# The second FFN's down product in another order: seven products, a weight sum by VectorE, a ring of its own for plain blocks, and later transposes

## The chip, the cores and the metric

The kernel runs on one core of a Trainium2 chip. The core has five engines that work side by side, each with an in-order queue of its own: TensorE (PE: matmuls; PEld is its loading of weights), VectorE (DVE), ScalarE (ACT), GpSimd (POOL) and SyncE (SP, which here only issues transfers). Sixteen DMA engines move data between the large memory and the on-chip memory; SP, ACT and POOL issue their transfers. The metric is the device time of one execution in microseconds (us), as the median of several runs.

## What is computed

Two layers of a diffusion backbone over 512 latent and 256 context tokens of width 1024, in float32. Each layer is a mixer (attention and linear recurrences) followed by a feed-forward network (FFN). The change is in the FFN of the second layer, in which only the 512 latent tokens are left. Cut to that:

```python
D_MODEL = 1024
SEQ = 512
D_FF = 2816

def _swiglu(h, w_gate, w_up, w_down):
    return (jax.nn.silu(h @ w_gate) * (h @ w_up)) @ w_down

def reference(...):
    ...
        h_lat = _modulate(_rms(x_lat, norm_pre_ffn[l]), m_lat[3], m_lat[4])
        x_lat = x_lat + m_lat[5] * _rms(_swiglu(h_lat, ffn_w_gate[l], ffn_w_up[l], ffn_w_down[l]), norm_post_ffn[l])
    ...
    return x_lat
```

## The kernel before

**Precision.** Every float32 operand of a matmul is split into a high part H (a cast by ScalarE to the matmul's reduced float32) and the rest L (a subtraction by VectorE). `mm3` then issues three matmuls, H·H, H·L and L·H. So each block of weights and of activations costs one ScalarE and one VectorE instruction before TensorE can use it.

**The second FFN** is `ffn_whole`. `first()` computes the first two columns of the gate and up products plainly, in two halves of 256 tokens (tiles "pearly"). While it does so, the last two token tiles are still being normed; their transposes wait in a list `self.turns`, and `self.turn(left)` issues transposes until `left` tiles are left. A tile's transposes are eight TensorE instructions (tile hT), each four followed by ScalarE's scale and shift and by the split into H and L. The tiles of the first half were transposed earlier, under the output projection; the two that wait belong to the second half of the tokens. After that, `seven` does the other gate and up products with a fast algorithm (seven products of half blocks in place of eight). The result is G, 512 tokens by 2816, in `np_` = 11 chunks of 2 times 128.

**The down product** is `down`: G (512 by 2816) times `w_down` (2816 by 1024), again with seven products of half blocks. A[r, k] are the four quarters of G (token half r, every other 128 rows k); B(k, j) those of the weights (half j of the columns). A[1, 0] has already had A[1, 1] taken off (`minus`). The products, each over 11 chunks, for two token tiles of 128 and 512 columns:

| name | activations (factor f) | weights (src) | bank before |
|---|---|---|---|
| 11 | A11 | B11 | X |
| N3 | A[0,0] as it then is, plus A12 | B22 | O |
| S1 | A21 − A22 | B11 + B12 | Q |
| SN | A21 − A22 − A11 | B11 + B12 + B22 | X, onto what 11 left |
| 22 | A22 | B11 + B12 + B22 + B21 | O |
| S3 | −A22 − (A21 − A22 − A11) | B12 + B22 | X, onto what 11 and SN left |
| 12 | A12 | B21 | Q |

The sums of weights are built in place in two tiles: `t` ("tb" in the profile) and `t3` ("tc"), each of 11 chunks of 512 columns. Where a sum grows, POOL issues an accumulating transfer (`add`, line 1707) from the large memory onto the tile, right after the operands of the product that used the old value were split. Plain blocks (N3, 12 and part of 11) go through a ring "raw" of three tiles that the whole kernel shares. The blocks of 11 for the first six chunks were loaded early (`early`).

The 11 chunks come in seven groups: two of one chunk, four of two, one of one. `operands(p, g)` makes H and L of weights and activations for a group; `ahead(3)` keeps three groups ready. The activations' ring (aH, aL) has three slots, that of the weights (wH, wL) four. After the last group of a product, each of its two output tiles is taken out of its bank into y, by ScalarE where it is the first term (`nc.scalar.copy`), by VectorE where it is added (`plus`, line 1761). `end` norms a finished token tile and stores it; `final` and `close` do the same for the last tile in two halves.

TensorE's matmuls in `down` and POOL's transfers there stay in the order of the program; what VectorE, ScalarE and SP do is ordered by a planner before the run, from the order of the program and from costs that it assumes. On the chip each queue is then in order.

Of the kernel before, what the change touches and what calls it, by code (L numbers as in the profile page):

```python
# [8 lines left out]
F32 = mybir.dt.float32  # L9
F32R = mybir.dt.float32r  # L10
# [3 lines left out]
ALU = mybir.AluOpType  # L14
# [3 lines left out]
P = 128  # L18
# [10 lines left out]
WU = 1024  # L29
# [104 lines left out]
class Attention:  # L134
# [7 lines left out]
    half = (slice(0, 64), slice(64, P))  # L142
# [174 lines left out]
class Net:  # L317
# [1295 lines left out]
    def ffn_whole(self, l, xp, yp, fp, pp, rp, h, ending):  # L1613


        nc, I = self.nc, self.I
        wg, wu, wd = I["ffn_w_gate"][l], I["ffn_w_up"][l], I["ffn_w_down"][l]
        tiles, n = h.order, h.n
        np_, nh = NFC // 2, n // P
        G = fp.tile([P, np_, 2, 2 * n], F32, tag="G", name="G")  # L1620

        self.banks(True)

        def go():
            return fp.tile([P, 2, 2 * n], F32, tag="go", name="go")

        def first():
            g = go()
            us = [[self.unit_cols(w, i * P) for w in (wg, wu)] for i in range(2)]
            h.open(xp)  # L1630
            for half in range(2):
                pm = self.mm_tile("pearly")
                pts = [[self.sc_tile("pearly", x)[:, :n] for x in range(2)], [pm[:, 512 * x : 512 * x + n] for x in range(2)]]
                tok = slice(n * half, n * half + n)
                for ks in ((range(4), range(4, 8)) if half == 0 else (range(8),)):
                    for i in range(2):
                        for m in range(2):
                            for k in ks:
                                self.mm3(pts[i][m], tuple(x[:, k, :] for x in us[i][m]), h.raw(k, half), k == 0, k == KD - 1)
                            if ks[0] == 0 and half == 0 and m == 0:  # L1640
                                self.turn(1 - i)
                for i in range(2):
                    nc.scalar.activation(g[:, i, tok], pts[i][0], AF.Silu)
                    nc.vector.tensor_tensor(G[:, 0, i, tok], g[:, i, tok], pts[i][1], op=ALU.mult)
                if half == 0:
                    pp.release()
                    tp = self.open_pool(f"t{l}")
                    h.sums(tp)
            h.late()
            return tp  # L1650

        tp = first()
        early = yp.tile([P, 8, 512], F32, tag="y", bufs=1, name="early")
        other = early[:, 6:8, :]
        self.blocks = wd.rearrange("(i k p) m -> k p i m", k=2, p=P)
        minus = lambda i: nc.vector.tensor_tensor(G[:, i, 0, n:], G[:, i, 0, n:], G[:, i, 1, n:], op=ALU.subtract)
# [24 lines left out]
        rp.release()  # L1681
        xp.release()
        dp = self.open_pool(f"d{l}")
        self.banks(None)
        y = self.down(dp, G, early, yp.tile([P, len(tiles), D], F32, tag="y", bufs=1, name=f"y{l}"), tiles, n, ending)
        return y

    def down(self, dp, G, early, y, tiles, n, ending):


        nc = self.nc
        np_, nh = NFC // 2, n // P
        B = lambda k, j, i: self.blocks[k][:, i, 512 * j : 512 * j + 512]
        A = {(r, k): G[:, :, k, n * r : n * r + n] for r in range(2) for k in range(2)}
        groups = [slice(0, 1), slice(1, 2)] + [slice(i, min(i + 2, np_)) for i in range(2, np_, 2)]
        ng = len(groups)
        v = nc.vector
# [6 lines left out]
        t = dp.tile([P, np_, 512], F32, name="tb")  # L1704
        t3 = dp.tile([P, np_, 512], F32, name="tc")
        end, final, follow = ending(y)
        add = lambda o, src: self.pin(nc.gpsimd.dma_start(out=o, in_=src, accum_op=ALU.add))
        load = lambda o, src: nc.sync.dma_start(out=o, in_=src)
        seven = (("11", "X"), ("N3", "O"), ("S1", "Q"), ("SN", "X"), ("22", "O"), ("S3", "X"), ("12", "Q"))

        def operands(p, g):
            i = groups[g]
            m = i.stop - i.start
            name = seven[p][0]
            H, L = [self.wp.tile([P, WU], F32R, tag=f"w{x}", bufs=4, name=f"w{x}")[:, : 512 * m].rearrange("p (i n) -> p i n", i=m) for x in "HL"]
            if name == "11":
                load(t[:, i], B(0, 0, i))
                if i.stop <= 6:
                    src = early[:, i]
            if name in ("N3", "12") or name == "11" and i.stop > 6:  # L1720
                src = self.wp.tile([P, WU], F32, tag="raw", bufs=3, name="raw")[:, : 512 * m].rearrange("p (i n) -> p i n", i=m)
                load(src, {"11": B(0, 0, i), "N3": B(1, 1, i), "12": B(1, 0, i)}[name])
            elif name != "11":
                src = (t3 if name == "S3" else t)[:, i]
            a = [x[:, :m] for x in (first.pop() if first else ring())]
            if name == "N3":
                f = dp.tile([P, 2, n], F32, tag="n3", bufs=2, name="n3")[:, :m]
                v.tensor_tensor(f, A[0, 0][:, i], A[0, 1][:, i], op=ALU.add)
            elif name == "S3":
                f = A[1, 1][:, i]  # L1730
                v.scalar_tensor_tensor(f, f, -1.0, A[0, 0][:, i], op0=ALU.mult, op1=ALU.subtract)
            else:
                f = A[{"11": (0, 0), "S1": (1, 0), "SN": (0, 0), "22": (1, 1), "12": (0, 1)}[name]][:, i]
            nc.scalar.copy(H, src)
            nc.scalar.copy(a[0], f)
            v.tensor_tensor(L, src, H.bitcast(F32), op=ALU.subtract)
            v.tensor_tensor(a[1], f, a[0].bitcast(F32), op=ALU.subtract)
            if name == "11":
                v.tensor_tensor(f, A[1, 0][:, i], f, op=ALU.subtract)
                add(t[:, i], B(0, 1, i))  # L1740
            elif name == "S1":
                add(t[:, i], B(1, 1, i))
                self.pin(nc.gpsimd.dma_start(out=t3[:, i], in_=B(0, 1, i)))
            elif name == "SN":
                add(t[:, i], B(1, 0, i))
                add(t3[:, i], B(1, 1, i))
            return a, (H, L)

        todo = [(p, g) for p in range(7) for g in range(ng)]
# [8 lines left out]
        out = {"X": [one(f"x{i}") for i in range(2)], "O": [one(f"o{i}") for i in range(2)]}  # L1758
        out["Q"] = [self.sc_tile("q", i) for i in range(2)]
        low, high = slice(0, 512), slice(512, D)  # L1760
        plus = lambda o, b, op=ALU.add: v.tensor_tensor(o, o, b, op=op)
        for p, (name, where) in enumerate(seven):
# [4 lines left out]
            for at, (g, i) in enumerate(order):  # L1767
# [3 lines left out]
                b = out[where][i]  # L1771
# [14 lines left out]
                y0, y1 = y[:, i, :], y[:, nh + i, :]  # L1786
                if name == "11":
                    nc.scalar.copy(y0[:, low], b)
                elif name == "N3":
                    nc.scalar.copy(y0[:, high], b)  # L1790
                elif name == "S1":
                    nc.scalar.copy(y1[:, high], b)
                    plus(y0[:, high], b)
                elif name == "SN":
                    plus(y0[:, high], b, ALU.subtract)
                elif name == "22":
                    nc.scalar.copy(y1[:, low], b)
                elif name == "S3":
                    plus(y1[:, low], b)
                    plus(y1[:, high], b, ALU.subtract)  # L1800
                    end(y1, tiles[nh + i])
                    if i == nh - 1:
                        close = final(dp, y0, tiles[i])
                else:
                    plus(y0[:, low], b)
                    if i < nh - 1:
                        end(y0, tiles[i])
                    else:
                        close()
# [304 lines left out]
```

## Time and profile before

| | us |
|---|---|
| median of three runs | 1743.5 (1741.79 to 1743.84) |
| the profiled execution's own time | 1742.7 |
| its span, first to last instruction | 1740.9 |
| TensorE busy | 1675.3 (96% of the span) |
| VectorE busy | 1298.3 (75%) |
| ScalarE busy | 896.4 (51%) |
| GpSimd busy | 108.6 (6%) |
| down product of the second FFN, first to last matmul | 1597.2 to 1733.1 |
| `first()` of the second FFN, first to last matmul | 1363.0 to 1394.5 |

How to read a row of the profile: a row of the time line gives start, duration, engine, line of the kernel, operation, the tile written <- the tiles read, their shape, and in brackets the idle time of the engine before it and what ended it. A row of the waits gives who waited for whom: us in total, times, the longest. A row by stretches gives the stretch, its length, the busy time (and instructions) of PE, PEld, DVE, ACT and POOL, the granted TensorE clock (1.00 is full speed), the mean busy share of the 16 DMA engines and GB/s. A group's row gives busy us, mean ns of one, and idle time before them. Matmuls overlap in the pipeline, so a row's duration is longer than the time from one start to the next.

### The profile page before, as it was taken

Reading aid. Unit: us, or ns where it says so; the run is one execution under the profiler, and the core shown is the slowest. Engines: PE = TensorE matmul, PEld = TensorE weight load, DVE = VectorE, ACT = ScalarE, POOL = GpSimd, SP = SyncE. Lnnn points to the kernel's source line nnn. Section 1 sums busy time; section 2 is a strip of 40 time slices with the busy share of each in tenths; the row PEclk is TensorE's granted clock in tenths of the full one; section 3 lists DMA queues with packets and bytes.
Section 4 is the critical chain, followed back from the end, with each engine's and each line's share of the span. In section 5 each row is a group of like instructions: output and inputs, shape, how many; then the busy total and the mean of one; then the engine's idle time right before and its main releaser. Section 6 shows DMA issues by size and latency. Waiting matters only on the chain.

```text
span 1740.9 us, 32512 instructions
## 1 busy us (share of the span) xinstructions
PE 1675.3 (96%) x13446; PEld 1500.4 (86%) x13446; DVE 1298.3 (75%) x2103; ACT 896.4 (51%) x1552; POOL 108.6 (6%) x128
## 2 busy tenths in 40 slices
PE   6999999999999999999999999999999999999887
PEld 5899987887999988999997888888887899998665
DVE  5889668835969999796668238887855789886667
ACT  4745567746442323333347346666644755554454
POOL 1004110000000000000001000000000000001240
PEclk9999999999999999999999999999999999999999
DMA  9641022134334455452235121211224253334993
GB/s 319 197 139 39 2 70 82 58 134 145 109 95 127 151 185 175 138 171 73 62 108 182 61 85 50 62 44 44 62 84 141 79 158 111 108 98 139 239 191 115
DMA packets 179680, 201.64 MB, mean 116 GB/s; under 512 B 7142, under 2 KB 141836, under 8 KB 179532
## 3 DMA queue, kind: packets, MB, share of 16 engines
q1 hardware_dynamic: 170704, 181.56, 33.3%
q0 software_dynamic: 6896, 14.42, 4.1%
q10 hardware_dynamic: 1932, 3.59, 0.7%
q8 instruction: 105, 1.72, 0.4%
q14 instruction: 43, 0.35, 0.1%
HBM read 190.08 MB, written 9.46 MB: 115 GB/s over the span
## 4 chain that ended last, share of the span: by engine, by line
PE 77%; DVE 9%; DMA 6%; ACT 4%; issue 2%; POOL 1%; SPq 0%; POOLq 0%; DVEq 0%; ACTq 0%
PE nat L355 12%; PE a L355 10%; PE acc L355 8%; PE ff L355 8%; PE E L355 7%; PE oproj L355 5%; PE D L355 3%; PE b L355 3%; PE fq L355 2%; PE gqk L355 2%; PE S L355 1%; PE pearly L355 1%; DMA tb<-in_ffn_w_down_dram 1%; DMA raw<-in_ffn_w_down_dram 1%; PE poh L355 1%
## 5 line engine op out<-in xcount | busy, mean ns | idle before, releaser
L355 PE MATMUL nat<-wH,x 128*128 128x256 f32 (+2 forms) x944 | 215.6, 318 | 3.0 <-ACT x L648 2.6
L734 ACT CAST wH<-raw 128x1024 fp32r<-128x1024 f32 x120 | 125.1, 1052 | 181.2 <-PE acc L355 54.1
L680 DVE TENSOR_TENSOR wL<-raw,wH 128x1024 fp32r<-128x1024 f32 (+1 forms) x104 | 124.3, 1203 | 82.5 <-ACT wH L679 81.6
L355 PEld LDWEIGHTS nat<-wH,x 128*128 128x128 f32 x944 | 157.6, 190 | 18.5 <-ACT x L648 3.6
L735 DVE TENSOR_TENSOR wL<-raw,wH 128x1024 fp32r<-128x1024 f32 x120 | 145.9, 1220 | 30.4 <-ACT wH L734 30.0
L679 ACT CAST wH<-raw 128x1024 fp32r<-128x1024 f32 (+1 forms) x104 | 106.8, 1038 | 81.1 <-PE nat L355 23.7
L355 PE MATMUL nat<-wL,x 128*128 128x256 f32 (+2 forms) x472 | 148.5, 315 | 0.0
L607 POOL TENSOR_TENSOR rs<-ms,neghalf 128x1 f32<-128x1 f32 (+2 forms) x62 | 57.8, 934 | 1278.4 <-DVE ms L605 1278.1
L537 DVE SCALAR_TENSOR_TENSOR macc<-mraw,scT,macc 128x1024 f32<-128x1024 f32 x98 | 122.7, 1278 | 8.1 <-DMA mraw<-in_mod_w_dram 7.8
L355 PE MATMUL ff<-x,wH 128*128 128x512 f32 (+1 forms) x512 | 127.6, 340 | 0.0
L355 PE MATMUL acc<-wH,gH 128*128 128x512 f32 x264 | 104.6, 397 | 1.3 <-DVE y L826 0.8
L355 PE MATMUL acc<-wL,gH 128*128 128x512 f32 x264 | 103.2, 391 | 1.4 <-DVE wL L680 1.4
L355 PE MATMUL acc<-wH,gL 128*128 128x512 f32 x264 | 103.2, 391 | 0.0
L355 PE MATMUL oproj<-wH,x 128*128 128x512 f32 x320 | 101.8, 395 | 0.5 <-ACT x L1241 0.4
L355 PEld LDWEIGHTS ff<-x,wH 128*128 128x128 f32 x512 | 87.4, 190 | 10.1
L355 PEld LDWEIGHTS nat<-wL,x 128*128 128x128 f32 x472 | 89.8, 190 | 5.1
L929 ACT COPY qkh<-arr 128x512 f32<-128x512 f32 x112 | 70.1, 642 | 36.3 <-DVE arr L934 32.2
L355 PE MATMUL ff<-x,wL 128*128 128x256 f32 (+1 forms) x256 | 86.2, 337 | 0.0
L826 DVE TENSOR_TENSOR y<-y,acc 128x512 f32<-128x512 f32 (+1 forms) x81 | 68.9, 861 | 22.4 <-PE acc L355 21.1
L759 DVE TENSOR_TENSOR raw<-raw 128x512 f32<-128x512 f32 x120 | 82.5, 688 | 2.0
L934 DVE TENSOR_TENSOR arr<-arr,f 128x512 f32<-128x512 f32 x112 | 74.2, 686 | 1.9 <-ACT qkh L929 0.3
L355 PE MATMUL a<-T,wH 128*128 128x384 f32 (+1 forms) x320 | 70.3, 309 | 0.7 <-ACT G L797 0.7
(411 smaller groups left out, 4428.5 us busy)
## 6 DMA issues: line engine op xcount, KB each, us to landing
mraw<-in_mod_w_dram SPq DMA_DIRECT2D x80, 512.0 KB, 4.0
raw<-in_ffn_w_gate_dram SPq DMA_DIRECT2D x44, 512.0 KB, 4.0
raw<-in_ffn_w_up_dram SPq DMA_DIRECT2D x44, 512.0 KB, 4.6
raw<-in_odd_w_in_dram SPq DMA_DIRECT2D x40, 512.0 KB, 3.8
raw<-in_ffn_w_down_dram SPq DMA_DIRECT2D x32, 512.0 KB, 3.8
mraw<-in_mod_w_dram SPq DMA_DIRECT2D x32, 256.0 KB, 6.4
raw<-in_even_w_in_dram SPq DMA_DIRECT2D x16, 512.0 KB, 3.7
x<-xr SPq DMA_DIRECT2D x14, 512.0 KB, 2.6
```

The lines of the kernel that those rows point to most:

```text
L355: return self.pin(self.nc.tensor.matmul(*a, **k))
L537: nc.vector.scalar_tensor_tensor(a, u, w, a, op0=ALU.mult, op1=ALU.add)
L607: nc.gpsimd.tensor_tensor(rs, ms, self.neghalf.to_broadcast([P, w]), op=ALU.pow)
L679: nc.scalar.copy(H[:, :m], raw[:, :m])
L680: nc.vector.tensor_tensor(L[:, :m], raw[:, :m], H[:, :m].bitcast(F32), op=ALU.subtract)
L734: self.nc.scalar.copy(H, f)
L735: self.nc.vector.tensor_tensor(L, f, H.bitcast(F32), op=ALU.subtract)
L759: add = lambda o, x, y: nc.vector.tensor_tensor(o, x, y, op=ALU.add)
L826: nc.vector.tensor_tensor(y, y, pt, op=ALU.add)
L929: nc.scalar.copy(qkv[:, :, :, half, :], dst)
L934: nc.vector.tensor_tensor(dst, dst, tb, op=ALU.mult)
```

## The change

It has two places. In `first()`, the two waiting tiles' transposes are issued at other points. With (chunk, i, m) for the chunk's first k, the column and gate or up: before, the first tile's followed (0, 0, 0) and the second's (0, 1, 0), that is, 12 and 36 matmuls into the half. After, the first follows (0, 1, 0) and the second (4, 0, 1), 36 and 72 matmuls in.

```diff
-                            if ks[0] == 0 and half == 0 and m == 0:
-                                self.turn(1 - i)
+                            if half == 0 and (ks[0], i, m) in ((0, 1, 0), (4, 0, 1)):
+                                self.turn(1 - ks[0] // 4)
```

In `down`, the order becomes 11, S1, N3, SN, S3, 22, 12, on banks X, O, Q, X, X, O, Q. The tile t is no longer loaded with B11 and grown by B12 in a transfer: B12 is loaded into t3 by SP, and VectorE writes t = B11 + B12 from the block of 11 and t3. With that the copy of B12 into t3 goes as well. The add of B22 into t3 moves from SN to N3. The blocks of N3 and 12 get a ring of their own with four slots. The subtraction that turns A[0, 0] into A21 − A22 − A11 moves from 11 to S1, and S3's factor goes to a ring tile ("n3") instead of over A22.

```diff
-        seven = (("11", "X"), ("N3", "O"), ("S1", "Q"), ("SN", "X"), ("22", "O"), ("S3", "X"), ("12", "Q"))
+        seven = (("11", "X"), ("S1", "O"), ("N3", "Q"), ("SN", "X"), ("S3", "X"), ("22", "O"), ("12", "Q"))
...
+            if name == "11" and i.stop <= 6:
+                src = early[:, i]
+            elif name == "11":
+                src = shape(self.wp.tile([P, WU], F32, tag="raw", bufs=3, name="raw"))
+                load(src, B(0, 0, i))
+            elif name in ("N3", "12"):
+                src = shape(dp.tile([P, WU], F32, tag="raw", bufs=4, name="rawd"))
+                load(src, B(1, 1, i) if name == "N3" else B(1, 0, i))
+            else:
+                src = (t3 if name == "S3" else t)[:, i]
             if name == "11":
-                load(t[:, i], B(0, 0, i))
-                if i.stop <= 6:
-                    src = early[:, i]
-            if name in ("N3", "12") or name == "11" and i.stop > 6:
-                src = self.wp.tile([P, WU], F32, tag="raw", bufs=3, name="raw")[:, : 512 * m].rearrange("p (i n) -> p i n", i=m)
-                load(src, {"11": B(0, 0, i), "N3": B(1, 1, i), "12": B(1, 0, i)}[name])
-            elif name != "11":
-                src = (t3 if name == "S3" else t)[:, i]
+                load(t3[:, i], B(0, 1, i))
...
             elif name == "S3":
                 f = A[1, 1][:, i]
-                v.scalar_tensor_tensor(f, f, -1.0, A[0, 0][:, i], op0=ALU.mult, op1=ALU.subtract)
+                x = dp.tile([P, 2, n], F32, tag="n3", bufs=2, name="s3")[:, :m]
+                v.scalar_tensor_tensor(x, f, -1.0, A[0, 0][:, i], op0=ALU.mult, op1=ALU.subtract)
+                f = x
...
             if name == "11":
-                v.tensor_tensor(f, A[1, 0][:, i], f, op=ALU.subtract)
-                add(t[:, i], B(0, 1, i))
+                v.tensor_tensor(t[:, i], src, t3[:, i], op=ALU.add)
             elif name == "S1":
+                x = A[0, 0][:, i]
+                v.tensor_tensor(x, f, x, op=ALU.subtract)
                 add(t[:, i], B(1, 1, i))
-                self.pin(nc.gpsimd.dma_start(out=t3[:, i], in_=B(0, 1, i)))
+            elif name == "N3":
+                add(t3[:, i], B(1, 1, i))
             elif name == "SN":
                 add(t[:, i], B(1, 0, i))
-                add(t3[:, i], B(1, 1, i))
...
-                elif name == "N3":
-                    nc.scalar.copy(y0[:, high], b)
                 elif name == "S1":
                     nc.scalar.copy(y1[:, high], b)
+                    nc.scalar.copy(y0[:, high], b)
+                elif name == "N3":
                     plus(y0[:, high], b)
                 elif name == "SN":
                     plus(y0[:, high], b, ALU.subtract)
+                elif name == "S3":
+                    nc.scalar.copy(y1[:, low], b)
+                    plus(y1[:, high], b, ALU.subtract)
                 elif name == "22":
-                    nc.scalar.copy(y1[:, low], b)
-                elif name == "S3":
                     plus(y1[:, low], b)
-                    plus(y1[:, high], b, ALU.subtract)
                     end(y1, tiles[nh + i])
```

More of the change, by code (lines that the diff above doesn't have):

```diff
@@ L1714, in operands @@
             name = seven[p][0]
-            H, L = [self.wp.tile([P, WU], F32R, tag=f"w{x}", bufs=4, name=f"w{x}")[:, : 512 * m].rearrange("p (i n) -> p i n", i=m) for x in "HL"]
-            if name == "11":
-                load(t[:, i], B(0, 0, i))
-                if i.stop <= 6:
-                    src = early[:, i]
-            if name in ("N3", "12") or name == "11" and i.stop > 6:
-                src = self.wp.tile([P, WU], F32, tag="raw", bufs=3, name="raw")[:, : 512 * m].rearrange("p (i n) -> p i n", i=m)
-                load(src, {"11": B(0, 0, i), "N3": B(1, 1, i), "12": B(1, 0, i)}[name])
-            elif name != "11":
-                src = (t3 if name == "S3" else t)[:, i]
+            shape = lambda x: x[:, : 512 * m].rearrange("p (i n) -> p i n", i=m)
+            H, L = [shape(self.wp.tile([P, WU], F32R, tag=f"w{x}", bufs=4, name=f"w{x}")) for x in "HL"]
+            if name == "11" and i.stop <= 6:
[8 more added lines that the diff above has]
+                src = (t3 if name == "S3" else t)[:, i]
+            if name == "11":
+                load(t3[:, i], B(0, 1, i))
             a = [x[:, :m] for x in (first.pop() if first else ring())]
```

## The prediction

> **What bounds the kernel now.** I read the page first, then the busy times by stretch of the stage that the change touches (one stretch for each of the seven products, cut where TensorE's output changes bank), then the waits of that stage, then single rows of the time line.
>
> ```profile
> span 1740.9 us, 32512 instructions
> ```
> ```profile
> core 0: us, PE busy (x) PEld busy (x) DVE busy (x) ACT busy (x) POOL busy (x), PEclk, DMA share, GB/s
> 1597.23:1616.41 19.18, 16.74 (x68) 13.43 (x67) 15.39 (x28) 6.39 (x11) 7.12 (x7) 0.91 1.04 302
> 1616.41:1640.24 23.83, 18.13 (x67) 13.17 (x66) 13.57 (x20) 11.88 (x20) 2.65 (x5) 0.93 0.83 230
> 1640.24:1655.20 14.96, 14.96 (x67) 12.39 (x66) 10.48 (x14) 9.79 (x18) 8.13 (x10) 1.00 1.05 234
> 1655.20:1670.21 15.01, 15.01 (x68) 12.31 (x66) 11.92 (x18) 8.75 (x15) 9.03 (x10) 1.00 1.10 246
> 1670.21:1694.22 24.01, 18.39 (x67) 12.06 (x66) 11.13 (x16) 9.21 (x15) 7.81 (x7) 1.00 0.99 180
> 1694.22:1711.89 17.67, 15.88 (x68) 12.15 (x66) 14.52 (x23) 10.45 (x18) 0.00 (x0) 1.00 0.16 47
> 1711.89:1733.08 21.19, 17.00 (x67) 13.18 (x65) 17.54 (x24) 9.98 (x17) 1.98 (x3) 0.92 0.44 148
> ```
>
> The rows are the products 11, N3, S1, SN, 22, S3 and 12. Each has 66 matmuls; S1 and SN run without a gap in 15.0 us, or 0.227 us a matmul, so 15.0 is what a product costs. The others lose 4.2 (11), 8.8 (N3), 9.0 (22), 2.7 (S3) and 6.2 us (12): 30.9 us in all, which is everything that a reordering could win here. The waits say for what:
>
> ```profile
> ACT wH L1734 <- DMA tb<-in_ffn_w_down_dram: 20.0, 8, 3.6
> ACT wH L1734 <- DMA raw<-in_ffn_w_down_dram: 18.1, 7, 4.0
> PE o L355 <- ACT aH L1735: 9.6, 7, 3.7
> PE x L355 <- DVE aL L1737: 4.1, 3, 2.4
> PE q L355 <- DVE wL L1736: 2.9, 1, 2.9
> ```
>
> N3 and 22 are the two products that write bank o, and behind ScalarE's lateness stands a transfer: for N3 the raw block that shares a ring of three, for 22 the weight sum tb. After a long gap the clock costs more:
>
> ```profile
> 1624.10 0.80 PE L355 MATMUL o<-wH,aH 128*128 128x512 f32 x1 [3.65 <-ACT aH L1735]
> 1624.69 0.63 PE L355 MATMUL o<-wL,aH 128*128 128x512 f32 x1
> ```
>
> 0.43 us from row to row in place of 0.227: half speed. Three of the products (granted clock 0.91, 0.93, 0.92) show it, each losing some 1.6 us. The Trainium skill (TensorE: Matmul & The Clock Gate, Part 1: The HAM clock gate) says that the clock halves after an idle window of about 3.4 us and takes as long to return; the stretch of product 12 has a drop with a longest listed wait of 2.9 us, so here a shorter gap was enough. By the page alone the 1.6 us of product 12 would not be in its loss.
>
> **The change part by part.** *Transfers.* For each of seven groups the load of t goes, a load of t3 of the same size comes on SP; on POOL the add of B12 into t and the copy of B12 into t3 go, two of five. What that frees:
>
> ```profile
> q0 software_dynamic: 6896, 14.42, 35.7%
> q1 hardware_dynamic: 12648, 17.23, 25.5%
> ```
>
> This is the queue table from 1540 to 1741 us. 35.7% of 201 us is 71.8 us of all 16 engines for POOL's 14.42 MB (201 GB/s), 14.4 us for one set of seven; SP's 17.23 MB take 51.3 us (336 GB/s). In the first five products the DMA share sums to 95.7 us over 97.0 us: the engines were full. Two sets less leave 67 us against 75 us of matmuls. So transfers stop being the limit of the stage, if with little to spare.
>
> *Order.* Every sum now has a whole product (15.0 us) between its add and its use; before, tb's add after SN was wanted at once in 22. N3's blocks come third, from a ring of four that nothing else uses.
>
> ```profile
> DMA to landing us min/median/max: 5.6/8.1/14.8
> DMA to landing us min/median/max: 3.7/4.5/13.9
> ```
>
> These are the landings of tb and of raw: the worst, 14.8, is still under 15.0. So I set 22 at 0.5 us lost (0 to 0.5). For N3 the adds into t3 (14.4) and three late ring loads (1.31 MB at 336 GB/s, 3.9) want 18.3 us of engines within its 15.0: between 0 and 4.3 lost (the excess and one more), I take 1.0, nearer the end without a wait, as four of the seven groups are there before. The Trainium skill (DMA: Bandwidth & Descriptors, Issuing engines are not separate DMA queues) speaks against the ring: whoever issues, all runs on the same 16 engines, so four early blocks would push the loads of t3 back; the shares near 1.0 agree, and my estimate by that rule is the upper end that follows for product 11.
>
> *Product 11* keeps its 4.2: the wait for aL stands behind the last gate products. New is that VectorE waits for t3, and aL of the next group is queued behind the sum.
>
> ```profile
> SPq L1708 <- PE E L355: 17.5, 1, 17.5
> 1595.88 3.89 SPq L1708 DMA_DIRECT2D tb<-in_ffn_w_down_dram  x7
> 1603.36 1.21 POOL L1707 DMA_DIRECT2D tb<-in_ffn_w_down_dram  x1 [0.34 <-DMA tb<-in_ffn_w_down_dram]
> ```
>
> The third group of tb landed 7.5 us after the first issue. t3 lies behind tb, on places that the last product of the stage before frees at 1597.2 (first row of the stretches), 1.3 us later. The ring's first four blocks, 1.57 MB, may go ahead (4.7 us). Operands are made three groups ahead, which hides some 3 us. So 0 to 3.0 more; I take 0.8: 5.0.
>
> *VectorE.* The seven sums are new; nearest are the seven splits of tc, of the same shapes. The seven subtractions move from 11 to S1.
>
> ```profile
> L1736 DVE TENSOR_TENSOR wL<-tc,wH 128x1024 fp32r<-128x1024 f32 (+1 forms) x7 | 6.9, 984 | 0.0
> L1739 DVE TENSOR_TENSOR G<-G 128x512 f32<-128x512 f32 (+1 forms) x7 | 3.9, 567 | 0.0
> L1761 DVE TENSOR_TENSOR y<-y,x 128x512 f32<-128x512 f32 x6 | 3.8, 681 | 0.0
> ```
>
> +6.9 us in the stage. In S1 a pair group needs 1.2 (wL), 0.68 (aL) and 0.68 (subtraction), 2.6 us against 12 matmuls of 0.227, 2.7: it fits, with 0.4 over at three single groups in a row. S1: 0.5, from 0 to 2.5 if two sums of 0.98 spill over. The number of evacuations stays (ten adds, eight copies); S3's factor goes to a ring of two instead of overwriting A22, which 22 now reads later; no cost, it is what N3 does already.
>
> *A new wait.* SN and S3 now follow each other in the same bank x, so S3 must wait until VectorE has taken SN out.
>
> ```profile
> 1670.12 0.42 DVE L1731 SCALAR_TENSOR_TENSOR G<-G 128x256 f32<-128x256 f32 x1
> 1670.47 1.28 DVE L1761 TENSOR_TENSOR y<-y,x 128x512 f32<-128x512 f32 x2
> ```
> ```profile
> 1670.21 0.39 PE L355 MATMUL o<-wH,aH 128*128 128x512 f32 x1
> ```
>
> Before, product 22 started at 1670.21 while VectorE emptied x from 1670.47 to 1671.75; S3 in its place would have waited for the first half, to 1671.1: 0.9. Bounds: 0.3 (VectorE free when the first tile ends), 2.1 (behind a split of 1.2). I take 1.0. Behind it on TensorE's queue stands all of S3. Of S3's old 2.7 (aL late, VectorE catching up after 22) I leave 1.0 of 0 to 2.7. S3: 2.0 (0.3 to 4.8).
>
> *Product 12.* VectorE closes two tiles first:
>
> ```profile
> 1711.41 1.88 DVE L1761 TENSOR_TENSOR y<-y,x 128x512 f32<-128x512 f32 x3
> 1714.59 0.68 DVE L1761 TENSOR_TENSOR y<-y,x 128x512 f32<-128x512 f32 x1
> 1716.62 1.22 DVE L1736 TENSOR_TENSOR wL<-raw,wH 128x1024 fp32r<-128x1024 f32 x1
> 1718.95 0.68 DVE L1737 TENSOR_TENSOR aL<-G,aH 128x512 fp32r<-128x512 f32 x1
> ```
>
> Two of the four adds are now done after S3, so wL and aL come 1.3 us earlier; the wait of 2.9 shrinks below what dropped the clock, 1.6 more. 6.2 becomes 3.3; bounds 1.5 and 6.2 (nothing won).
>
> *Later transposes.* In the second FFN's first products the last tile's transposes (hT) stand in TensorE's queue before its norm is ready:
>
> ```profile
> 1364.43 1.04 PE L358 MATMUL hT<-ident,xn 128*128 128x128 f32 x8
> 1372.32 1.09 PE L358 MATMUL hT<-ident,xn 128*128 128x128 f32 x4 [3.99 <-DVE xn L624]
> ```
> ```profile
> 1371.42 0.75 DVE L624 TENSOR_SCALAR xn<-xr,rs 128x1024 f32<-128x1024 f32 x1 [0.73 <-POOL rs L607]
> 1380.38 0.42 DVE L1644 TENSOR_TENSOR G<-go,pearly 128x256 f32<-128x256 f32 x1 [2.91 <-PE pearly L355]
> 1381.86 0.69 DVE L98 TENSOR_TENSOR x<-f,x 128x512 fp32r<-128x512 f32 x1
> ```
> ```profile
> 1363.00:1383.36 20.36, 16.37 (x117) 16.19 (x116) 14.07 (x19) 14.70 (x30) 1.10 (x2) 0.83 0.42 130
> 1383.36:1394.52 11.16, 11.16 (x96) 11.16 (x95) 11.12 (x14) 5.41 (x8) 0.00 (x0) 1.00 0.12 34
> ```
>
> The 96 matmuls of the second token half take 11.16 us, 0.116 each. Now the last transposes follow 72 matmuls and the other tile's eight transposes: 1363.0 + 8.4 + 1.0 is 1372.4, just when xn is there. 4.0 us of gap and some 2.4 of half clock go, 6.4 at most. But the second half needs the last split, at 1381.86, and VectorE is then busy to the end of the stretch; it can come forward only by its own idle 2.91. I take 3.0, from 0 to 6.4.
>
> **Sum.** Lost after: 5.0 + 0.5 + 1.0 + 0 + 2.0 + 0.5 + 3.3 = 12.3 (11, S1, N3, SN, S3, 22, 12), 18.6 less than 30.9. With 3.0, 21.6 off the profiled execution's 1742.7 us: 1721.1. That execution lies 0.8 under the median of the runs, so 1722 us. All lower bounds: 6.0 lost and 6.4 won, 31.3 off, 1712. All upper bounds: 7.2 + 2.5 + 4.3 + 0 + 4.8 + 0.5 + 6.2 = 25.5 lost and nothing from the transposes, 5.4 off, 1738.
>
> **Rivals.** *VectorE takes the transfers' place:* its queue is in order, and the seven sums, waiting for t3, lie on the path with all their 6.9 us: 1729. For it: 15.39 busy of 19.18 us in product 11. Against it: 94.6 of 135.9 us busy over the seven stretches, rows summed. *POOL's order keeps 22's wait:* the add of B21 stands in POOL's queue behind the adds into t3, so 22 loses its 9.0 again, 8.5 more: 1730. For it: DMA shares at 1.0. Against it: S3's 15 us now lie between. *Slower: the transfers stay the limit.* If the loads of t3 crawl as N3's blocks did, VectorE's queue stops on them and product 11 takes on N3's 8.8 (13.0), N3 keeps its 8.8 for its last ring loads, 22 keeps 9.0, S3 and 12 stand at 4.8 and 6.2, S1 0.5: 42.3, 11.4 more than now, less 3.0: 1752. It decides where t3's last group lands after the first product should end (1616). For it: the full engines; against it: 28.7 us less to carry.
>
> **How the numbers follow.** Forecast 0.72, VectorE 0.12, POOL's order 0.08, transfers 0.08. The first two rivals at once would end near 1737; a quarter of VectorE's share, 0.03, I put within 0.2% of before (3.5 us, about what a measurement of this kernel can tell from no change). So faster 0.89, the same 0.03, slower 0.08. The range, 1712 to 1738, is the forecast's own; it holds both fast rivals and leaves out the slow one and some of the ends.
>
> **What would show it.** Right: no gap over 2 us in bank o's products; ScalarE's waits for tb and raw near zero instead of 38.1; SN and S3 together at 31 to 33 us; VectorE at 101 us over the seven stretches (94.6 + 6.9); no gap before hT. Wrong: VectorE waiting for tc in product 11 by more than 3 us, the second product over 17.5 us, or the last of the FFN's first products ending no earlier than the 1394.52 of the stretch above.

## The result and the profile after

The changed kernel takes 1720.74 us (median of four runs, 1718.93 to 1725.09) beside 1743.67 us for the kernel before on the same chip: a ratio of 0.9871, 95% interval 0.9848 to 0.9895. The forecast was 1722. The profiled execution took 1719.44 us.

The page of the changed kernel, its span and its busy times:

```profile
span 1717.5 us, 32485 instructions
PE 1665.1 (97%) x13446; PEld 1494.9 (87%) x13446; DVE 1301.8 (76%) x2110; ACT 894.8 (52%) x1552; POOL 96.8 (6%) x114
```

TensorE is busy 10.2 us less than the 1675.3 of before, so a part of the time won was within the rows and not between them. The down product by stretches, cut as in the prediction, but for SN and S3, which now write the same bank and are cut at 1659.40, ahead of S3's wait for it (columns: PE, PEld, DVE, ACT, POOL, granted clock, DMA share, GB/s); the rows are now 11, S1, N3, SN, S3, 22 and 12:

```profile
1592.41:1611.28 18.87, 15.77 (x68) 12.26 (x67) 17.21 (x26) 8.21 (x15) 0.27 (x1) 1.00 0.90 317
1611.28:1626.34 15.06, 15.06 (x68) 12.31 (x66) 15.06 (x26) 9.78 (x17) 8.63 (x9) 1.00 0.90 152
1626.34:1644.40 18.06, 16.33 (x67) 12.07 (x66) 13.19 (x22) 10.79 (x20) 6.22 (x6) 1.00 1.09 251
1644.40:1659.40 15.00, 15.00 (x67) 12.17 (x65) 12.43 (x19) 8.86 (x15) 6.06 (x6) 1.00 1.12 229
1659.40:1675.44 16.04, 15.25 (x68) 12.50 (x67) 13.61 (x21) 9.26 (x15) 1.43 (x2) 1.00 0.45 83
1675.44:1690.47 15.03, 15.03 (x67) 12.31 (x66) 11.82 (x17) 9.78 (x18) 0.00 (x0) 1.00 0.20 54
1690.47:1709.66 19.19, 16.87 (x67) 12.85 (x65) 16.08 (x22) 9.88 (x17) 2.50 (x3) 0.91 0.39 137
```

Against 15.0 us each, the products lose 3.9 (11), 0.1 (S1), 3.1 (N3), 0 (SN), 1.0 (S3), 0 (22) and 4.2 (12): 12.3 in all where it was 30.9. The stage is 18.6 us shorter. The waits of that stage (who waited for whom: us in total, times, longest):

```profile
ACT wH L1740 <- DMA rawd<-in_ffn_w_down_dram: 5.8, 3, 2.5
PE x L355 <- DVE aL L1743: 3.1, 2, 2.4
PE q L355 <- DVE aL L1743: 2.3, 2, 1.9
DVE tb L1745 <- DMA tc<-in_ffn_w_down_dram: 1.7, 2, 1.1
PE q L355 <- ACT aH L1741: 1.6, 1, 1.6
PE x L355 <- DVE y L1768: 0.8, 1, 0.8
```

ScalarE no longer waits for a weight sum. Of its 38.1 us behind transfers 5.8 are left, all in N3. VectorE waits 1.7 us for t3, under the 3 that would have spoken against the forecast. The 0.8 is the new wait of S3 on its bank, the two rows on aL are VectorE's lateness in 11 and 12, as before, and the 1.6 on aH is in N3, behind its late blocks.

`first()` in the changed kernel, by stretches (the cut at 1377.16 is the first matmul of the second token half, the last one the start of the next stage):

```profile
1361.26:1377.16 15.90, 14.11 (x115) 13.47 (x113) 11.60 (x16) 11.34 (x26) 1.10 (x2) 1.00 0.54 166
1377.16:1388.32 11.16, 11.15 (x91) 11.03 (x92) 11.11 (x13) 7.69 (x11) 0.00 (x0) 1.00 0.01 1
1388.32:1388.73 0.41, 0.41 (x5) 0.41 (x5) 0.41 (x1) 0.22 (x1) 0.00 (x0) 1.00 0.00 0
```

And single rows of its time line on TensorE:

```profile
1372.26 0.66 PE L358 MATMUL hT<-ident,xn 128*128 128x128 f32 x4 [0.16 <-ACT f L638]
...
1377.16 0.39 PE L355 MATMUL pearly<-x,wH 128*128 128x256 f32 x1 [1.14 <-DVE x L98]
...
1425.17 0.50 PE L355 MATMUL a<-T,wH 128*128 128x256 f32 x2 [1.73 <-ACT G L797]
```

The gap of 3.99 before hT is 0.16, and the clock is 1.00 where it was 0.83. The price is the gap of 1.14 ahead of the second half, where VectorE's last split is late. The part takes 27.47 us, before 31.52 (1363.00 to 1394.52): 4.05 won. 1.0 of it goes back before the down product starts (203.68 us from 1388.73 to 1592.41, before 202.71 from 1394.52 to 1597.23), most of it in the wait of 1.73 (before 0.67).

So the two profiled executions, 1742.7 and 1719.4, differ by 23.3 us: 18.6 from the down product, 3.1 from the transposes, and 1.7 that lie ahead of `first()`, in code that both share. That much is variation between executions: in the runs below that change nothing ahead of the down product, it starts between 1590.46 and 1595.30.

### The profile page after: what moved, and what is told of

It is laid out like the page before. It is cut to its first block, busy times and chain, and to the rows that moved or that the text cites. A ratio compares the mean times of both kernels' runs of the same rounds, so it can differ in the third digit from the quotient of the medians.

```text
span 1717.5 us, 32485 instructions
## 1 busy us (share of the span) xinstructions
PE 1665.1 (97%) x13446; PEld 1494.9 (87%) x13446; DVE 1301.8 (76%) x2110; ACT 894.8 (52%) x1552; POOL 96.8 (6%) x114
## 4 chain that ended last, share of the span: by engine, by line
PE 77%; DVE 11%; DMA 5%; ACT 4%; issue 2%; POOL 1%; ACTq 0%; DVEq 0%; POOLq 0%; SPq 0%
PE nat L355 12%; PE a L355 10%; PE acc L355 8%; PE ff L355 8%; PE E L355 7%; PE oproj L355 5%; PE b L355 3%; PE D L355 3%; PE fq L355 3%; PE x L355 2%; PE gqk L355 2%; DMA mraw<-in_mod_w_dram 2%; DVE macc L537 2%; PE o L355 2%; PE S L355 1%
```

## The experiments

For the runs, the kernel before was run again on the same chip; its medians were 1741.3 to 1741.9. Ratios are to that. Product times are read like the rows above.

### The parts by themselves

**The later transposes alone.** The kernel before, with the two lines of `first()`:

```diff
-                            if ks[0] == 0 and half == 0 and m == 0:
-                                self.turn(1 - i)
+                            if half == 0 and (ks[0], i, m) in ((0, 1, 0), (4, 0, 1)):
+                                self.turn(1 - ks[0] // 4)
```

> The kernel before with the later transposes alone. My theory: the gap of 4.0 us before the last tile's transposes goes and its half clock with it, but the second token half then waits for VectorE's splits, and about 1 us is given back at the first wait of the steady stage; net 3.1 us, so about 1740.5 us, and the down product's stretch stays at 135.9 us. Rival A: the stage is paced by VectorE and the weight loads anyway, so the gap only moves and the time stays at 1743.5 (within 0.5 us). Rival B: the gap costs all its price, 6.4 us: 1737.

Measured: 1740.01 us, ratio 0.9989 [0.9978, 0.9999]. `first()` takes 27.32 us, so the 4 us are won there. The stage after it takes 203.39, 0.7 more than before. In its down product, which is the code of before, this execution took 138.08 where the one shown takes 135.85; the difference is product 22 (26.47 beside 24.01). By the runs the part is worth 0.2 to 3.8 us.

**The ring alone,** in the old order:

```diff
-                src = self.wp.tile([P, WU], F32, tag="raw", bufs=3, name="raw")[:, : 512 * m].rearrange("p (i n) -> p i n", i=m)
+                pool, bufs = (self.wp, 3) if name == "11" else (dp, 4)
+                src = pool.tile([P, WU], F32, tag="raw", bufs=bufs, name="raw")[:, : 512 * m].rearrange("p (i n) -> p i n", i=m)
```

> The kernel before, old order, with the plain blocks of N3 and 12 in a ring of four of their own. My theory: N3's loss of 8.8 us came from blocks that could not be asked for before the shared ring had room, so it falls to about 3 to 4 us as in the changed kernel (3.1), while 22 keeps its 9.0; about 1738.5 us. Rival: the 16 DMA engines were full in this stretch (share 0.83 to 1.04), so earlier requests only queue and delay tb; N3 keeps 8 us or more or hands it to S1, and the time stays within 1 us of 1743.5.

Measured: 1741.0 us, 0.9998 [0.9987, 1.0009]. N3 takes 23.08 us (23.83 before), 22 takes 23.38, the rest is as it was. More places in the on-chip memory bring nothing in the old kernel; the rival is right.

**The changed kernel without the ring:**

```diff
-                src = shape(dp.tile([P, WU], F32, tag="raw", bufs=4, name="rawd"))
+                src = shape(self.wp.tile([P, WU], F32, tag="raw", bufs=3, name="raw"))
```

> The changed kernel with N3's and 12's blocks back in the shared ring of three. My theory: N3, now third, can have three of its seven groups early and waits for the other four: its loss goes from 3.1 to 6 to 8 us and the time from 1720.7 to about 1725. Rival: the new order alone brings the gain, because as the third product N3 has 15 us more for its loads; then the time stays within 1 us of 1720.7. Rival B: without the ring's early loads in front, t3 lands sooner and product 11 gets back part of its 3.9.

Measured: 1724.91 us, 0.9910 [0.9895, 0.9925]; N3 21.99 us, the whole stage 121.44. In the changed kernel the same ring is worth 3.9 us in N3 and 4.2 in the stage, and product 11 gets nothing back without it (19.37). Whether the new place of N3 or the fewer transfers make the ring useful is not separated: no run puts N3 alone back to its old place.

**The weight sum by a transfer again.** The changed kernel, with t loaded and B12 added by POOL as before; t3 is still loaded:

```diff
+                load(t[:, i], B(0, 0, i))
                 load(t3[:, i], B(0, 1, i))
...
-                v.tensor_tensor(t[:, i], src, t3[:, i], op=ALU.add)
+                add(t[:, i], B(0, 1, i))
```

> The changed kernel, but t is loaded with B11 and grown by B12 in POOL's accumulating transfer as before; VectorE makes no weight sums. My theory: S1, now second, follows its add at once, as 22 did before, and loses 5 to 9 us, and two more sets of seven transfers (2.9 MB each) fill the engines again, so N3's 3.1 grows; about 1729 us. Rival: VectorE's 6.9 us for the sums cost as much as they save; then the time is at or under 1720.7.

Measured: 1731.4 us, 0.9946 [0.9931, 0.996]; the stage takes 126.48 us, 9.2 more. Nearly all of it is in S1, the second row of the stretches of this kernel:

```profile
1593.31:1611.17 17.86, 15.42 (x68) 12.42 (x67) 15.65 (x29) 7.40 (x14) 4.35 (x4) 1.00 1.01 307
1611.17:1635.15 23.98, 18.96 (x67) 12.94 (x66) 11.32 (x16) 10.74 (x18) 8.68 (x8) 0.93 1.09 290
```

Its waits over these two products:

```profile
POOL tb L1707 <- DMA tb<-in_ffn_w_down_dram: 18.9, 6, 5.4
ACT wH L1741 <- DMA tb<-in_ffn_w_down_dram: 13.1, 5, 4.8
```

This is a chain: POOL's add waits for the load of t, and ScalarE waits for the add. Product 11 is 1.0 us shorter without VectorE's sums (17.86 beside 18.87), so by these two executions the sums cost about that; in the other executions with the sums product 11 took 18.16 to 19.47. The run carries two sets more, and both fall in these two products, so the chain and the number of transfers are not taken apart here.

### What 22 waited for

The prediction says that 22 recovers because every sum now has a whole product between its add and its use, while tb's add after SN was wanted at once.

**22 directly behind SN.** The changed kernel with S3 and 22 in their old order:

```diff
-... ("SN", "X"), ("S3", "X"), ("22", "O"), ("12", "Q"))
+... ("SN", "X"), ("22", "O"), ("S3", "X"), ("12", "Q"))
...
-                elif name == "S3":
-                    nc.scalar.copy(y1[:, low], b)
-                    plus(y1[:, high], b, ALU.subtract)
                 elif name == "22":
+                    nc.scalar.copy(y1[:, low], b)
+                elif name == "S3":
                     plus(y1[:, low], b)
+                    plus(y1[:, high], b, ALU.subtract)
```

> The changed kernel with S3 and 22 swapped, so that 22 follows SN at once as before; all else is kept (VectorE's sums, the ring, fewer transfers). My theory: 22 waits for the add of B21 that SN's operands have just released, whatever else the engines carry, because one add takes 8 us from issue to landing; it loses 6 to 9 us, and the wait of S3 for the bank (0.8) goes: about 1728. Rival: with 28.7 us less to carry the adds land at once, 22 loses under 2 us, and the time stays within 1.5 us of 1720.7: then the bytes were the cause in product 22, not the order.

Measured: 1722.79 us, 0.9899 [0.9882, 0.9916]. The last three products by stretches are 22, S3 and 12:

```profile
1659.30:1674.26 14.96, 14.96 (x67) 12.39 (x66) 12.63 (x19) 8.97 (x15) 1.22 (x2) 1.00 0.48 88
1674.26:1689.22 14.96, 14.96 (x67) 12.39 (x66) 12.44 (x19) 9.88 (x17) 0.00 (x0) 1.00 0.18 50
1689.22:1711.23 22.01, 18.12 (x67) 13.87 (x65) 17.44 (x24) 9.88 (x18) 1.97 (x3) 0.84 0.34 122
```

22 loses nothing though its sum is grown right ahead of it. So the whole product between add and use is not what 22 needs here, and the reason given for it falls; whether it would be enough where SN issues two adds a group, no run shows. What the changed kernel has from the exchange of S3 and 22 is elsewhere: product 12 takes 19.19 in place of 22.01, since VectorE has two adds into y fewer ahead of it (the 1.3 us of the prediction and what hangs on them), against 1.0 for the bank in S3.

**Two adds behind SN.** The run above, with the add into t3 put back from N3 to SN:

```diff
-            elif name == "N3":
-                add(t3[:, i], B(1, 1, i))
             elif name == "SN":
                 add(t[:, i], B(1, 0, i))
+                add(t3[:, i], B(1, 1, i))
```

> The swapped kernel (SN, 22, S3) with the add of B22 into t3 back behind SN's operands, beside the add of B21 into t, as before the change; the bytes of the stage stay the same. The swap alone left product 22 without a loss, so my first theory, that an add needs a whole product between issue and use, has fallen. New theory: what 22 waited for was the pace of two adds for each group. One add of 0.5 MB takes 2.6 us at 201 GB/s, two 5.2, against 2.7 us of matmuls; so with both behind SN, 22 stops again at each pair group every 5 us and loses 7 to 9 us: about 1730. Rival: the fewer bytes of the whole stage are enough (POOL's transfers stay 21), so 22 still loses under 2 us: 1722 to 1724.

Measured: 1721.48 us, 0.9891 [0.9874, 0.9907]; 22 takes 19.18 us, 4.2 lost, less than was expected and about half of what it lost before. ScalarE's splits of tb for two of 22's groups in this kernel:

```profile
1661.15 1.05 ACT L1740 CAST wH<-tb 128x1024 fp32r<-128x1024 f32 x1 [3.54 <-DMA tb<-in_ffn_w_down_dram]
...
1666.21 1.05 ACT L1740 CAST wH<-tb 128x1024 fp32r<-128x1024 f32 x1 [3.50 <-DMA tb<-in_ffn_w_down_dram]
```

And in the run above, with one add behind SN:

```profile
1663.22 1.05 ACT L1740 CAST wH<-tb 128x1024 fp32r<-128x1024 f32 x1 [0.97 <-DMA tb<-in_ffn_w_down_dram]
1665.79 1.05 ACT L1740 CAST wH<-tb 128x1024 fp32r<-128x1024 f32 x1 [0.99 <-DMA tb<-in_ffn_w_down_dram]
```

With two adds a group the splits are 5.1 us apart, with one 2.6. POOL starts an add about every 2.5 us there (tc at 1656.29, tb at 1658.89, tc at 1661.38), so the second add of a group, which the next product does not want, stands on POOL's queue ahead of the next group's add, which it does want. Whether POOL's queue or the 16 engines behind it set this pace, the runs do not separate. The kernel as a whole shows no loss by it: N3, free of these adds, takes 15.55 us beside 17.52 in the run above, and 1721.48 us is no more than 1722.79. What moving the add wins in 22 is by these rows half paid back in N3, and in the time of the kernel it does not show.

**S1's second set as well.** To see whether the other half is a backlog that S1's two sets leave, S1 issues its second transfer again, a copy of B12 over the same B12 in t3:

```diff
                 add(t[:, i], B(1, 1, i))
+                self.pin(nc.gpsimd.dma_start(out=t3[:, i], in_=B(0, 1, i)))
```

> 22 right behind SN, with two adds behind SN as before, lost 4.2 us in the run with two adds, against 9.0 before. Here S1 gets back its second transfer set on POOL (a copy of B12 over the same B12 in t3, which changes no value), so that S1 and SN again issue two sets each. Theory (the rest of 22's loss is backlog from S1): the first add of SN is issued more than 1 us after SN's first matmul, and 22 takes 23 to 25 us; N3 stands between S1 and SN now, so some 14.4 us of POOL's transfers have N3's 15 us to drain and N3's late blocks land later, N3 17 to 21 us; total 1727 to 1732. Rival (the backlog of S1 has nothing to do with it): 22 stays at 19 us, total 1721 to 1725.

Measured: 1725.61 us, 0.9908 [0.9887, 0.9929]. The stretches of SN and 22 in this kernel:

```profile
1644.60:1659.57 14.97, 14.97 (x68) 12.39 (x67) 11.49 (x17) 8.88 (x15) 6.82 (x7) 1.00 1.10 190
...
1659.57:1678.30 18.73, 17.41 (x68) 13.45 (x66) 11.79 (x18) 9.18 (x15) 5.26 (x5) 0.91 0.83 150
```

POOL's last transfer of S1 and first add of SN on its time line:

```profile
1628.57 1.42 POOL L1750 DMA_DIRECT2D tc<-in_ffn_w_down_dram  x1
1641.70 0.86 POOL L1707 DMA_DIRECT2D tb<-in_ffn_w_down_dram  x1 [11.71 <-ACT wH L1740]
```

The same two on the time line of the kernel before, where SN starts at 1655.20:

```profile
1655.76 1.39 POOL L1743 DMA_DIRECT2D tc<-in_ffn_w_down_dram  x1
1657.47 0.85 POOL L1707 DMA_DIRECT2D tb<-in_ffn_w_down_dram  x1 [0.31 <-issue]
```

22 still loses only 3.7. The theory expected 23 to 25 us there and a late first add; neither came, so the number of S1's transfers alone is not the other half. But the backlog was not restored: with N3 between S1 and SN POOL was idle for 11.7 us and issued SN's first add 2.9 us before SN's first matmul. Before, with SN directly behind S1, S1's transfers ran into SN and the first add came 2.3 us after its first matmul. With equal sets in S1 and in SN, 22 thus loses 3.7 where N3 stands between them and 9.0 where it does not. That is what these runs hold against each other; the two kernels differ in the sum by VectorE as well, which lies in product 11, over 30 us ahead of SN, and in the ring, with which alone 22 took 23.38. A kernel with S1 and SN adjacent and one set in S1 was not tried, so the part of the adjacency, some 5 us, rests on the rows of POOL and is not separated further. The rows do agree in size: SN's first add comes 5.2 us earlier against SN's start, and 22 loses 5.3 us less. In the two other executions with the old order, later transposes alone and ring alone, that add comes 2.65 and 1.79 us after SN's first matmul and 22 loses 11.5 and 8.4; in the run with two adds it comes 1.74 us ahead, and 22 loses 4.2. Over these five the loss grows with POOL's lateness.

The copy was not free here. Beside the run with two adds, N3 takes 19.28 us in place of 15.55 (ScalarE waits 5.4 us for its blocks in place of 2.1) and the median is 4.1 us higher, though the intervals of the ratios overlap.

**One set more in the changed kernel.** The same copy in the changed kernel itself, nothing else:

> The changed kernel with a second copy of B12 over the same B12 in t3 after S1 (no value changes): one set of POOL transfers more, 67 us of engines become 81 in 75 us of matmuls of the first five products. If the transfers are again the limit, the adds into t3 after N3 come late and SN or S3 or 22 lose 5 to 9 us between them, total 1726 to 1732. If the order alone has removed the limit, no more than N3's late blocks move, up to 2 us, total 1720 to 1723.

Measured: 1720.19 us, 0.9870 [0.9852, 0.9887], the time of the changed kernel. The second to fifth product by stretches (S1, N3, SN, S3):

```profile
1614.44:1629.40 14.96, 14.96 (x68) 12.39 (x66) 14.93 (x26) 9.80 (x17) 8.40 (x10) 1.00 0.95 208
1629.40:1647.07 17.67, 16.08 (x67) 12.08 (x66) 13.00 (x21) 10.79 (x20) 7.60 (x8) 1.00 1.08 298
1647.07:1662.06 14.99, 14.99 (x67) 12.19 (x65) 12.46 (x19) 8.87 (x16) 6.83 (x7) 1.00 1.12 229
1662.06:1678.06 16.00, 15.21 (x67) 12.50 (x67) 13.58 (x21) 9.23 (x15) 4.02 (x4) 1.00 0.91 165
```

The DMA share of S3 goes from 0.45 to 0.91, so POOL's transfers simply end a product later, and nothing wants them there. In this order the set was free, where the same copy cost 3.7 us in N3 in the kernel above. So a set has no price of its own: it costs where a product waits for it, or for a transfer that it delays.

### What is left, and a faster version

**N3's last three blocks.** The changed kernel lets N3's groups from the fifth on use the shared ring, which is idle by then:

```diff
-                src = shape(dp.tile([P, WU], F32, tag="raw", bufs=4, name="rawd"))
+                if name == "N3" and g >= 4:
+                    src = shape(self.wp.tile([P, WU], F32, tag="raw", bufs=3, name="raw"))
+                else:
+                    src = shape(dp.tile([P, WU], F32, tag="raw", bufs=4, name="rawd"))
```

> The changed kernel with N3's last three groups in the shared ring, idle by then, so that all seven of its blocks can be asked for early. My theory: N3's 3.1 us come from the last three loads, which wait for a slot and then land in 8.5 us among POOL's adds; asked for 10 us earlier they are there in time, N3 loses under 1 us: about 1718.4. Rival: the engines are full in this stretch, so the earlier loads only push t3's or t's transfers back, and the 3 us stay or move to product 11 or SN.

Measured: 1717.05 us, 0.9862 [0.9847, 0.9877]. N3 by stretches in this kernel:

```profile
1628.87:1644.05 15.18, 15.18 (x68) 12.31 (x67) 13.25 (x21) 10.70 (x20) 5.88 (x6) 1.00 1.08 246
```

The loss of N3 is gone at the same DMA share (1.08, in the changed kernel 1.09). In the changed kernel the three loads could not be issued before a place came free; on ScalarE's time line the first two land late:

```profile
1632.80 1.05 ACT L1740 CAST wH<-rawd 128x1024 fp32r<-128x1024 f32 x1 [2.51 <-DMA rawd<-in_ffn_w_down_dram]
...
1636.67 1.05 ACT L1740 CAST wH<-rawd 128x1024 fp32r<-128x1024 f32 x1 [2.30 <-DMA rawd<-in_ffn_w_down_dram]
```

and on SP's the issue is 8.6 us before the first of them:

```profile
1624.24 4.43 SPq L1708 DMA_DIRECT2D rawd<-in_ffn_w_down_dram  x3
```

**12 ahead of S3.** The order 11, S1, N3, SN, 12, S3, 22, with the ends of the tiles y0 and y1 exchanged, so that 12 does not follow a closing:

```diff
-... ("S3", "X"), ("22", "O"), ("12", "Q"))
+... ("12", "Q"), ("S3", "X"), ("22", "O"))
```

> The changed kernel in the order 11, S1, N3, SN, 12, S3, 22: the first token half closes after 12, the second after 22. S3 no longer follows SN in the same bank. My theory: product 12's 4.2 us come from VectorE's work of closing two tiles just ahead of it; that work now falls on S3's first groups and costs about the same there, so only the bank's 0.8 us is won: 1718 to 1721. Rival: what is lost in 12 is the wait for its own blocks or for its a ring; then it goes with 12 off the end, 3 us or more won: under 1718.

Measured: 1721.32 us, 0.9878 [0.9863, 0.9894]. 12 takes 14.96 and S3 20.00. Closing the first token tiles costs VectorE's time wherever it stands; here it falls ahead of S3's operands.

**22 in the order of the tail.** In the last product the last three groups run tile by tile, so that the first tile is closed earlier. The same for 22:

```diff
-            if p == 6:
+            if p >= 5:
```

> The changed kernel with product 22's last three groups done tile by tile, as 12's already are: the first of its two tiles ends 15 matmuls (3.4 us) before the second. My theory: VectorE then closes the first tile while TensorE is still in 22, so the waits at the start of 12 (1.9 and 0.4 and the half clock behind them, 4.2 in all) shrink by 2 us or more: about 1718.5. Rival: the operands of 12 are what is late, since the ring of three for the activations is held longer by the tail; then 12 loses as much or more, 1721 or over.

Measured: 1718.88 us, 0.9875 [0.986, 0.9891]. 12 takes 18.41, 0.8 less than in the changed kernel: two waits of 0.66 and 1.29 us for one of 1.89 and one of 0.43. The theory expected 2 us or more.

**Both.**

> The changed kernel with both edits that helped alone: N3's last groups in the idle shared ring (N3 lost 0.2 us in place of 3.1) and product 22's tail tile by tile (12 lost 3.4 in place of 4.2). Theory: they act on different products and add up: the down stretch falls from 117.25 to about 114 us, and the time to 1716 or 1717. Rival: the tail holds the rings longer and gives the 0.8 us back in 12, so it is no better than the slots alone (1717.05).

Measured: 1717.85 us, 0.9864 [0.985, 0.9879]; N3 15.19, 12 18.41, the stage 113.71 us, the shortest of all. Both kernels with N3's seven places have the lowest medians, faster than the kernel before, and by the ratios 1.2 to 1.6 us faster than the changed one (0.0007 and 0.0009 of 1743). The intervals of the ratios overlap with the changed kernel's, so that last step is shown by the rows of N3 and not by the runs.

## Why the prediction was right, and where it was not

The size was right: 18.6 us for the stage, the same 12.3 lost, and 3.1 beside 3.0 for the transposes. That the seven terms add up to the same 12.3 is luck: the misses are −1.1, −0.4, +2.1, −1.0, −0.5 and +0.9 and cancel.

- **Product 11**, 5.0 taken, 3.9 measured. VectorE's wait for t3 is 1.7 us in all and hides in the wait that was there; product 11 keeps its old 4.2, less a little. That VectorE would carry the sums on its path is refuted by 18.87, and its 99.4 us over the seven stretches (rows summed) are close to the 101 named. The two rows that the prediction shows for the half clock are 0.59 us apart; its 0.43 is the step of the rows behind them (1624.69, 1625.12, 1625.55).
- **S1**, 0.5 taken, 0.1 measured. Busy 15.06 of 15.06 us, VectorE fits with nothing over.
- **N3**, 1.0 taken, 3.1 measured: the largest miss, inside its bounds (0 to 4.3). The mechanism of the bound, late ring loads, was right; taking 1.0 because "four of the seven groups are there before" counted the groups that are early and not the three that must wait for a place.
- **SN and S3**, 31.04 us, the 31 to 33 that were named. S3 was taken as 2.0 and lost 1.0: the 1.0 left of its old wait for aL is gone, and the bank wait is 0.79, taken as 1.0:

```profile
1660.36 0.47 PE L355 MATMUL x<-wH,aH 128*128 128x512 f32 x1 [0.79 <-DVE y L1768]
```

- **22**, 0.5 taken, 0 measured, with a wrong reason. "Every sum now has a whole product between add and use" is not what it needs: without that cover it loses nothing either. What the runs show is that one add a group in place of two takes the loss from 4.2 to 0; that the rest of the 9.0 comes from POOL's late start on SN's adds is what its rows say, without a run that changes that alone. The change gives both, by moving the add of B22 to N3 and by putting N3 between S1 and SN. The rival that POOL's order keeps 22's wait had the right queue: with the order of adds of before, 3.7 to 4.2 of the 9.0 return.
- **Transfers**: "two sets less" was the right edit and the wrong account. The sum by VectorE is worth 9.2 us; the waits of its run say that it does so by cutting the chain from load to add to use, with the two sets that it saves not taken apart. One set on POOL can be put back at no cost in this order, with shares over five products of 81.5 us in 82.8 (each share of that run's stretches times its length, summed; the row of its product 11 stands in the last section). By a balance of engine time against matmuls (67 us against 75 in the prediction, 81 against 75 with the set put back) that run would have been slower.
- **Product 12**, 3.3 taken, 4.2 measured. The adds that are gone shorten its first wait from 2.9 to 1.89, 1.0 where 1.3 was worked out; the 1.6 us put down to a clock that would stay up did not come. The stretch still shows 0.91.
- **Transposes**: 3.1 of 6.4, limited by VectorE's last split, as argued. Not foreseen was that the next stage gives 1.0 of the 4.05 back.

## What to carry to other kernels

When the DMA engines are full, ask of each transfer who wants it next and how soon, not only how many there are. A load and an add on the chain from load to use went with 9.2 us; a copy that nobody waits for cost nothing in one order and 3.7 us in another, where it delayed blocks that were wanted. On an in-order queue that issues accumulating transfers, an add that is wanted soon loses by standing behind one that is not; but look at the product that takes the moved add too, since here it lost part of what the other won. That such a queue gains by a product of rest between two that load it is what POOL's rows suggest, not what a run of its own shows. More places in a ring brought nothing in the old kernel and 4.2 us in the changed one, and there every block that must wait for a place still counts.

## What the runs showed of the hardware

The half clock did not follow from the length of a gap, nor did it cost what its share suggests. After the same first gap in product 11, the changed kernel was granted 1.00 and the one with a copy more 0.91. The gap in the changed kernel:

```profile
1595.59 0.50 PE L355 MATMUL x<-wH,aL 128*128 128x512 f32 x1 [2.44 <-DVE aL L1743]
...
1599.31 0.50 PE L355 MATMUL x<-wH,aL 128*128 128x512 f32 x1 [0.66 <-DVE aL L1743]
```

Product 11 in the kernel with a copy more, whose first gap is 2.44 as well and which has no second one over 0.2:

```profile
1595.30:1614.44 19.14, 16.70 (x68) 13.39 (x67) 17.42 (x27) 8.31 (x15) 0.62 (x1) 0.91 0.88 311
```

The times are 18.87 and 19.14. Over the ten executions with the sum by VectorE product 11 took 18.16 to 19.01 us at 1.00 (three) and 19.14 to 19.47 at 0.91 (seven): 0.7 us between the means, where 0.09 of 19 us would be 1.7. In product 12 it is the other way round: 0.91 in the changed kernel with gaps of 1.89 and 0.43, 1.00 in the other with 1.90 and 1.65, and the times are 19.19 and 19.10. Nor does the drop stand at the gap: in the changed kernel's product 12 the rows after the gap are 0.23 us apart for another 1.5 us, and only then 0.43:

```profile
1695.70 0.50 PE L355 MATMUL q<-wH,aL 128*128 128x512 f32 x1 [1.89 <-DVE aL L1743]
...
1697.19 0.60 PE L355 MATMUL q<-wH,aL 128*128 128x512 f32 x1
1697.60 0.63 PE L355 MATMUL q<-wH,aH 128*128 128x512 f32 x1
1698.02 0.63 PE L355 MATMUL q<-wL,aH 128*128 128x512 f32 x1
```

In product 12 the half clock takes the place of waiting that would follow (a second gap of 0.43 there, 1.65 in the kernel with a copy more), so it must not be added in full to the gap as a cost of its own; the prediction did that in product 12. A DMA share of 1.12, in the stretch of SN, shows also that the share is not a bound that one can balance against to a few per cent.
